# Second mixture-of-experts layer: a routed job's transposes one job later, its down product two jobs later, and three dense slices ahead instead of four

## The chip, the cores and the metric

The kernel runs on one core of a Trainium2 chip. The time is device microseconds (us) of one execution; a kernel's time is the median of several runs. TensorE is written PE (its weight loads PEld), VectorE DVE, ScalarE ACT, GpSimd POOL, and SyncE, which issues the weight transfers, SP.

## The reference, cut to what matters

The whole reference is a stack of two two-layer blocks on 256 tokens of width 1024, in float32. Only its last stage is touched here: a mixture of eight SwiGLU experts of inner width 2816, of which each token uses its two best.

```python
def _moe_swiglu(x, router_w, w_gate, w_up, w_down):
    logits = (t @ router_w).astype(jnp.float32)
    top_vals, top_idx = lax.top_k(logits, TOP_K)          # TOP_K = 2
    w = jax.nn.softmax(top_vals, axis=-1)
    combine = jnp.einsum('nk,nke->ne', w, jax.nn.one_hot(top_idx, N_EXPERTS_2, ...))
    out = jnp.zeros_like(t)
    for e in range(N_EXPERTS_2):                          # 8 experts
        out = out + combine[:, e:e + 1] * _swiglu(t, w_gate[e], w_up[e], w_down[e])
# _swiglu: (silu(x @ w_gate) * (x @ w_up)) @ w_down
```

After it come the residual and a layer norm, and then the output.

## The kernel before, in words

`moe2` (L1621) does this stage. Each expert is cut into `NSL` = 11 slices of 256 inner columns. A slice needs three pieces of weights of 1 MB each: gate, up and down. A *job* is one slice of one expert, written `(r, s)`; there are 88 jobs, so 264 pieces.

Expert 0 is *dense*: it is computed for all 256 tokens (`r` is None). The other seven are *routed*: they are ranked at run time by how many tokens chose them (`route2`), and rank r is computed for a fixed number of gathered tokens. Ranks 0 to 2 (`HEAVY` = 3) take 128 tokens, rank 3 takes 64, ranks 4 to 6 (the *small* ones) take 32. What is left over is added in a branch at the end (`rest2`). Dense and heavy jobs split each weight half into a high and a low part (ACT at L102, DVE at L104, tile `whl`, a ring of six halves) and multiply three times; rank 3 and the small ones use the loaded weights as they are.

`jobs2` writes out the order of the jobs: `DENSE2` dense slices first, then the ranks in the order `SEQ2` = 4, 0, 5, 1, 6, 2, 3, with `AMONG2` dense slices spread among the slices of a rank: four among rank 4 and three among rank 5.

A job has three steps. `up` is the gate and up product with SiLU (ACT) and the product of the two (DVE; L1652 and L1653 for heavy ranks, L1662 and L1663 for the others, tile `sh`; L1372 and L1373 for a dense slice, tile `fh`). `hid`, for a routed job only, transposes the hidden rows on TensorE (L1672, L1681, L1683) and copies them out of PSUM (tiles `shh` and `shl`, or `lhT` at L1685). `down` is the down product into accumulators (tile `sy`, for a dense slice `fy`). Before, the loop issues for job j: `up(j)`, then the extra work tied to that slice, then `down(j-1)`, then `hid(j)`. The extra work is `scatter` of the rank before (slices 1 to 4, tile `scps`), `select` and `gather` for the next rank (slices 5, 7 and 8, tile `gps`), and `rows` (slice 6, tile `slps`).

The PSUM tiles of `up`, `hid`, `scatter`, `gather` and `rows` come from a pool `pg` of two banks that are handed out in turn (a dense `up` takes both). The tiles `fh`, `fhh` and `fhl`, which hold hidden rows and their transposes, have two buffers each.

Three things set the order of work. First, `chunks2` lists the weight pieces in the order in which the steps use them, and SP issues the loads in that order, through a ring of `N_RAW` = 12 buffers. Second, a routed expert's address needs its index: SP reads it at run time (`index2`, L1589), and waits there until `route2` has computed it (L1554). Third, the framework's scheduler fixes the order of instructions in each engine's queue when the kernel is built, from its own estimate of when each will be ready; it prefers the order of the code but fills what it takes for a wait with later work. On the chip each queue then runs strictly in that order.

Of the kernel before, what the change touches and what calls it, by code (L numbers as in the profile page):

```python
# [9 lines left out]
F32 = mybir.dt.float32  # L10
# [10 lines left out]
D = 1024  # L21
# [4 lines left out]
NSL = F2 // 256  # L26
# [3 lines left out]
POOL = tuple(map(int, "0021001000012221112220221210"))  # L30
LAG = 2

DENSE2, HEAVY, SMALL, CAP3 = 4, 3, 4, 32

SEQ2, AMONG2 = (4, 0, 5, 1, 6, 2, 3), (4, 0, 3, 0, 0, 0, 0)
RSQ = (1024 / 27) ** 2
BRANCH = [ET.PE, ET.DVE, ET.Activation, ET.SP]

# [185 lines left out]
class Kern:  # L224
# [1367 lines left out]
    def jobs2(self):  # L1592
# [6 lines left out]
                out.append((r, s))  # L1599
        return out  # L1600

    def chunks2(self, jobs):

        w = self.a["w_moe2"]

        def chunk(r, j):
            if r is None:
                return w[0, j], 2, False
            if callable(r):
                return w[r(), j], 2, False  # L1610
            return (lambda: w[bass.ds(self.index2(r), 1), j].rearrange("o p f -> (o p) f")), 2, r >= HEAVY

        c = []
        for i, (r, s) in enumerate(jobs):
            c += [chunk(r, 2 * s), chunk(r, 2 * s + 1)]
            if i:
                c.append(chunk(jobs[i - 1][0], 2 * NSL + jobs[i - 1][1]))
        c.append(chunk(jobs[-1][0], 2 * NSL + jobs[-1][1]))
        return c

    def moe2(self, stream, x, xt, began, ln, out):  # L1621
# [4 lines left out]
        with ExitStack() as st:  # L1626
# [37 lines left out]
                return h  # L1664

            def hid(r, s, h):
                if r is None:
                    return h
                if r < HEAVY:
                    ps = pg.tile([128, 2, 128], F32, name="shT", tag="fgu")  # L1670
                    for j in range(2):
                        nc.tensor.transpose(ps[:, j, :], h[:, half(j)], self.ident)  # L1672
                    hh = w2.tile([128, 2, 128], F32R, name="shh", tag="fhh")
                    hl = w2.tile([128, 2, 128], F32R, name="shl", tag="fhl")
                    self.split(hh, hl, ps)
                    return hh, hl
                n = size(r)
                ps = pg.tile([128, 2, n], F32, name="lT", tag="fgu")
                if r < SMALL:
                    for j in range(2):  # L1680
                        nc.tensor.transpose(ps[:, j, :], h[hi, half(j)], self.ident[hi, hi])  # L1681
                else:
                    nc.tensor.transpose(ps.rearrange("p j n -> p (j n)"), h[hi], self.ident[hi, hi])  # L1683
                hT = w2.tile([128, 2, n], F32, name="lhT", tag="fhh")
                nc.scalar.activation(hT, ps, AF.Copy)  # L1685
                return hT
# [40 lines left out]
            def select(r):  # L1727
                n = size(r)
                if r in small:
                    m = len(small)  # L1730
                    sel[r] = w2.tile([128, 2, m, n], F32, name="sel", tag="sel", bufs=1)
                    for t in range(2):
                        nc.vector.tensor_tensor(sel[r][:, t], self.iota[:, None, :n].to_broadcast([128, m, n]),
                                                pms[:, t, SMALL:, None].to_broadcast([128, m, n]), op=OP.is_equal)
                    sel[r] = sel[r].rearrange("p t m n -> p t (m n)")
                    t = w2.tile([128, 8, m * n], F32, name="xq", bufs=1)
                    for e in small:
                        xe[e] = t[:, :, half(e - SMALL, n)]
                    xe["small"] = t
                    return  # L1740
                sel[r] = w2.tile([128, 2, n], F32, name="sel", tag="sel", bufs=1)
                for t in range(2):
                    nc.vector.tensor_scalar(sel[r][:, t], self.iota[:, :n], pms[:, t, r:r + 1], None, op0=OP.is_equal)
                if r < HEAVY:
                    xe[r] = w2.tile([128, 8, 2, CAP2], F32R, name="xe", tag="xe", bufs=1)
                else:
                    xe[r] = w2.tile([128, 8, CAP1], F32, name="xl", tag="xl", bufs=1)

            def gather(r, q):
                n, m = sel[r].shape[-1], 4 if r < HEAVY or r in small else 8  # L1750
                ps = pg.tile([128, m, n], F32, name="gps", tag="fgu")
                for k in range(m):
                    for t in range(2):
                        self.mm(ps[:, k], x[:, t, half(m * q + k)], sel[r][:, t], t == 0, t == 1)
                v = xe["small" if r in small else r][:, half(q, m)]
                if r < HEAVY:
                    self.split(v[:, :, 0], v[:, :, 1], ps)
                else:
                    nc.scalar.activation(v, ps, AF.Copy)
# [10 lines left out]
            def scatter(r, t, c):  # L1770
                ps = pg.tile([128, 512], F32, name="scps", tag="fgu")
                for i in range(2):
                    spread(r, i, t, c, ps, i == 0)
                v = pre[:, t, half(c, 512)]
                nc.vector.tensor_tensor(v, v, ps, op=OP.add)

            pend = None
            for r, s in self.jobs2():
                if r == SEQ2[0] and s == 0:
                    select(r)  # L1780
                    for q in range(2):
                        gather(r, q)
                if r == last and s == 2:
                    gb = w2.tile([128, 2, D], F32, name="lngb", tag="xe", bufs=1)
                    gb = self.load_ln(ln, (gb[:, 0], gb[:, 1]), nc.scalar)
                h = up(r, s)
                b = before.get(r)
                b = "small" if b == small[-1] else None if b in small else b
                if b is not None and 1 <= s < 5:
                    scatter(b, (s - 1) // 2, (s - 1) % 2)  # L1790
                n = after.get(r)
                if n is not None and n not in small:
                    if s == 5:
                        select(n)
                    if s in (7, 8) and (n < HEAVY or s == 7):
                        gather(n, s - 7)
                if s == 6 and r is not None and r not in small[:-1]:
                    rows("small" if r in small else r)
                if r == last and s == 8:
                    bank = self.four(p0)  # L1800
                    for t in range(2):
                        for c in range(2):
                            self.mm(bank[t][c], self.ident, pre[:, t, half(c, 512)], True, False)
                if pend is not None:
                    down(*pend)
                pend = (r, s, hid(r, s, h))
            down(*pend)
            for i in range(2):
                for t in range(2):
                    for c in range(2):  # L1810
# [326 lines left out]
```

## Time and profile before

| | |
|---|---|
| median of three runs | 1993.34 us (1990.16 to 1996.72) |
| the profiled execution | 1993.39 us, with a span of 1991.6 us from its first to its last instruction |
| TensorE busy | 1866.9 us, 94% of the span |
| VectorE, ScalarE, GpSimd busy | 891.0, 732.0 and 302.5 us |
| bytes moved | 589.24 MB, 296 GB/s on average |
| TensorE's work in the second mixture-of-experts layer, from the second dense slice on | 1264.3 to 1973.4 us of the span |

Busy time of TensorE is modelled from pipelined matmuls, so a busy TensorE is not one at its peak. What a wait is worth depends on whether the weights or the products set the pace in that stretch, so the layer is read rank by rank.

### The profile page before, as it was taken

How to read it: one execution, taken by the hardware profiler on the slowest of the kernel's cores; microseconds unless marked ns; L12 is line 12 of the kernel's file. 1: busy time of each engine (PE TensorE's matmuls, PEld its weight loads, DVE VectorE, ACT ScalarE, POOL GpSimd, SP SyncE). 2: the span in 40 equal slices, each digit the busy share in tenths (PEclk: the TensorE clock that was granted, in tenths of full speed). 3: DMA queues.
4: the chain of work that ended last, by engine and by line, in shares of the span. 5: the costliest groups of instructions: out<-in, count | busy, mean ns of one | idle time of the engine just before them, and what ended most of it. 6: DMA issues, size and time to landing. Idle time of an engine off the chain costs nothing. (4 is left out here: it accounts for less than half of the span.)

```text
span 1991.6 us, 35592 instructions
## 1 busy us (share of the span) xinstructions
PE 1866.9 (94%) x14962; PEld 1470.1 (74%) x14962; DVE 891.0 (45%) x1609; ACT 732.0 (37%) x1177; POOL 302.5 (15%) x132
## 2 busy tenths in 40 slices
PE   9999999899999998998999999999999989979996
PEld 8885555488655555988999767988898779758953
DVE  5481111267411113476111576633586249628822
ACT  5431111054211112553444372533565247516611
POOL 0210000002000001524888234200000000000000
PEclk9899999999999998999999999999999999999998
DMA  9559999855598993744552431669998999999995
GB/s 383 194 202 402 408 419 419 327 193 191 196 412 328 371 419 117 283 186 158 191 189 94 181 115 64 254 258 389 419 388 312 407 419 388 351 418 419 378 384 208
DMA packets 86027, 589.24 MB, mean 296 GB/s; under 512 B 9782, under 2 KB 11510, under 8 KB 16340
## 3 DMA queue, kind: packets, MB, share of 16 engines
q1 hardware_dynamic: 83042, 580.67, 73.4%
q10 hardware_dynamic: 2802, 6.06, 0.9%
q8 instruction: 124, 2.03, 0.4%
q14 instruction: 59, 0.48, 0.1%
HBM read 585.45 MB, written 1.24 MB: 295 GB/s over the span
## 5 line engine op out<-in xcount | busy, mean ns | idle before, releaser
L102 ACT ACTIVATE whl<-raw 128x1024 fp32r<-128x1024 f32 x426 | 431.3, 1054 | 229.5 <-issue 104.2
L104 DVE TENSOR_TENSOR whl<-raw,whl 128x1024 fp32r<-128x1024 f32 x313 | 373.6, 1234 | 160.2 <-ACT whl L102 152.8
L104 POOL TENSOR_TENSOR whl<-raw,whl 128x1024 fp32r<-128x1024 f32 x113 | 278.1, 2478 | 902.4 <-ACT whl L102 819.1
L282 PE MATMUL fgu<-xh,whl 128*128 128x256 f32 x1280 | 234.8, 284 | 3.6 <-DVE whl L104 1.5
L282 PE MATMUL sgu<-whl,xe 128*128 128x256 f32 x1584 | 198.0, 284 | 10.4 <-ACT whl L102 5.8
L282 PEld LDWEIGHTS fgu<-xh,whl 128*128 128x128 f32 x1280 | 200.9, 192 | 6.0 <-DVE whl L104 1.9
L282 PEld LDWEIGHTS sgu<-whl,xe 128*128 128x128 f32 x1584 | 190.1, 191 | 13.7 <-ACT whl L102 6.9
L282 PE MATMUL fgu<-xl,whl 128*128 128x256 f32 x640 | 180.9, 283 | 0.0
L282 PE MATMUL gu<-raw,xe 128*64 128x256 f32 x1408 | 172.4, 382 | 0.0
L282 PEld LDWEIGHTS gu<-raw,xe 128*64 128x64 f32 x1408 | 102.0, 137 | 53.7 <-issue 5.1
L282 PEld LDWEIGHTS fgu<-xl,whl 128*128 128x128 f32 x640 | 122.8, 192 | 0.6
L282 PE MATMUL zps<-xh,whl 128*128 128x256 f32 x576 | 111.5, 291 | 2.2 <-ACT xh L271 1.4
L282 PE MATMUL fy<-whl,fhh 128*128 128x512 f32 x352 | 111.7, 398 | 0.0
L1860 POOL TENSOR_TENSOR pre<-pre,lngb 128x512 f32<-128x512 f32 x2 | 2.5, 1266 | 701.0 <-ACT pre L1859 701.0
L983 ACT ACTIVATE h<-gu 128x256 f32<-128x256 f32 x31 | 11.9, 385 | 253.6 <-PE gu L282 253.6
L1373 DVE TENSOR_TENSOR fh<-fh,fgu 128x512 f32<-128x512 f32 x20 | 13.8, 688 | 183.5 <-PE fgu L282 183.4
L984 DVE TENSOR_TENSOR h<-h,gu 128x256 f32<-128x256 f32 x31 | 13.1, 421 | 184.8 <-ACT h L983 184.8
L282 PEld LDWEIGHTS zps<-xh,whl 128*128 128x128 f32 x576 | 92.7, 195 | 3.9 <-ACT xh L271 1.6
L282 PE MATMUL yps<-raw,hT 128*64 128x512 f32 x352 | 89.5, 595 | 0.0
L282 PE MATMUL sy<-whl,shh 128*128 128x512 f32 x264 | 84.2, 402 | 3.6 <-ACT whl L102 2.5
L282 PE MATMUL zps<-xl,whl 128*128 128x256 f32 x288 | 82.6, 287 | 1.0 <-DVE xl L272 1.0
L282 PEld LDWEIGHTS fy<-whl,fhh 128*128 128x128 f32 x352 | 64.7, 188 | 15.9 <-issue 1.2
(469 smaller groups left out, 3049.4 us busy)
## 6 DMA issues: line engine op xcount, KB each, us to landing
raw<-in_w_moe_dram SPq DMA_DIRECT2D x399, 1024.0 KB, 9.7
whl<-in_w_moe_dram SPq DMA_DIRECT2D x57, 1024.0 KB, 10.9
raw<-in_w_dense_dram SPq DMA_DIRECT2D x53, 1024.0 KB, 7.1
raw<-in_w_ffn_dram SPq DMA_DIRECT2D x33, 1024.0 KB, 5.9
lngb<-in_lnp_dram ACTq DMA_DIRECT2D x8, 512.0 KB, 4.4
lngb<-in_lnp_dram SPq DMA_DIRECT2D x8, 512.0 KB, 5.1
xraw<-in_xT_dram SPq DMA_DIRECT2D x4, 256.0 KB
raw<-in_w_dense_dram SPq DMA_DIRECT2D x2, 512.0 KB, 4.5
```

The source lines that it names most:

```text
L102: nc.scalar.activation(hi, r, AF.Copy)
L104: on.tensor_tensor(lo, r, hi, op=OP.subtract)
L282: self.nc.tensor.matmul(out, lhsT, rhs, start=start, stop=stop, skip_group_check=True)
L983: nc.scalar.activation(h, ps[:, 0, :], AF.Silu)
L984: nc.vector.tensor_tensor(h, h, ps[:, 1, :], op=OP.mult)
L1373: nc.vector.tensor_tensor(h, h, g[1], op=OP.mult)
L1860: nc.gpsimd.tensor_tensor(v, v, gb[0][:, half(c, 512)], op=OP.mult)
```

## The change

The order of steps is now made by a new function, `steps2`, that both the loop and `chunks2` follow. For job j it issues: `up(j)`; then `down(j-2)` if that job was routed; then, for job j-1, `hid` if it is routed or `down` if it is dense; then the extra work of slice j (`more`). So a routed job's transposes come one job later than its gate and up product and its down product two jobs later; a dense slice's down product still comes one job later. The scatter of the rank before moves to slices 2 to 5. The weight pieces are loaded in the new order of use. The leading dense slices go from four to three, and four stand among rank 5 in place of three.

```diff
-DENSE2, HEAVY, SMALL, CAP3 = 4, 3, 4, 32
-SEQ2, AMONG2 = (4, 0, 5, 1, 6, 2, 3), (4, 0, 3, 0, 0, 0, 0)
+DENSE2, HEAVY, SMALL, CAP3 = 3, 3, 4, 32
+SEQ2, AMONG2 = (4, 0, 5, 1, 6, 2, 3), (4, 0, 4, 0, 0, 0, 0)
...
+    def steps2(self, jobs):
+        out, turned, last = [], None, None
+        for j in [*jobs, None, None]:
+            out += [("up", *j)] if j else []
+            out += [("down", *turned)] if turned else []
+            turned = None
+            if last is not None:
+                if isinstance(last[0], int):
+                    turned = last
+                out.append(("hid" if turned else "down", *last))
+            out += [("more", *j)] if j else []
+            last = j
+        return out
...
-        for i, (r, s) in enumerate(jobs):
-            c += [chunk(r, 2 * s), chunk(r, 2 * s + 1)]
-            if i:
-                c.append(chunk(jobs[i - 1][0], 2 * NSL + jobs[i - 1][1]))
-        c.append(chunk(jobs[-1][0], 2 * NSL + jobs[-1][1]))
+        for step, r, s in self.steps2(jobs):
+            if step == "up":
+                c += [chunk(r, 2 * s), chunk(r, 2 * s + 1)]
+            elif step == "down":
+                c.append(chunk(r, 2 * NSL + s))
...
-                if b is not None and 1 <= s < 5:
-                    scatter(b, (s - 1) // 2, (s - 1) % 2)
+                if b is not None and 2 <= s < 6:
+                    scatter(b, (s - 2) // 2, (s - 2) % 2)
...
-                if pend is not None:
-                    down(*pend)
-                pend = (r, s, hid(r, s, h))
-            down(*pend)
+            gb, bank, hidden = [], [], {}
+            for step, r, s in self.steps2(self.jobs2()):
+                if step == "up":
...
+                    hidden[r, s] = up(r, s)
+                elif step == "hid":
+                    hidden[r, s] = hid(r, s, hidden[r, s])
+                elif step == "down":
+                    down(r, s, hidden.pop((r, s)))
+                else:
+                    more(r, s)
```

## Rows read from the trace of the kernel before

**Rows 1.** The page: its span, and the loads of expert weights (size, landing).
```profile
span 1991.6 us, 35592 instructions
...
raw<-in_w_moe_dram SPq DMA_DIRECT2D x399, 1024.0 KB, 9.7
```

**Rows 2.** Busy time by stretch: length, PE, PEld, DVE, ACT, POOL, clock, DMA share, GB/s.
```profile
1264.30:1307.70 43.40, 43.40 (x298) 40.06 (x296) 20.39 (x19) 18.94 (x21) 7.29 (x3) 1.00 0.75 299
1307.70:1423.80 116.10, 112.69 (x1412) 96.92 (x1411) 39.60 (x49) 35.60 (x56) 0.00 (x0) 1.00 0.92 367
...
1525.70:1626.40 100.70, 93.20 (x1217) 77.59 (x1215) 36.48 (x49) 27.42 (x48) 0.00 (x0) 0.99 0.94 381
...
1725.90:1790.80 64.90, 48.58 (x934) 34.09 (x933) 14.80 (x32) 12.18 (x31) 0.00 (x0) 0.97 0.98 396
1790.80:1895.30 104.50, 101.29 (x729) 93.12 (x729) 85.81 (x93) 70.58 (x90) 0.00 (x0) 0.98 0.95 391
1895.30:1973.40 78.10, 74.79 (x496) 38.46 (x494) 12.53 (x23) 11.33 (x28) 0.00 (x0) 1.00 0.88 357
```

**Rows 3.** What SP waited for, 1190 to 1304 us: total, times, longest.
```profile
SPq L1589 <- DVE idxi L1554: 62.3, 1, 62.3
```

**Rows 4.** Busy time by stretches of 20 us, columns as in rows 2.
```profile
1290.00:1310.00 20.00, 20.00 (x195) 18.58 (x194) 8.86 (x10) 8.58 (x11) 0.00 (x0) 1.00 0.51 186
...
1790.00:1810.00 20.00, 16.04 (x118) 14.28 (x119) 13.34 (x14) 12.13 (x19) 0.00 (x0) 0.91 1.01 419
```

**Rows 5.** Timeline of DVE among the leading dense slices: start, length, instruction.
```profile
1282.43 0.68 DVE L1373 TENSOR_TENSOR fh<-fh,fgu 128x512 f32<-128x512 f32 x1
...
1299.53 0.68 DVE L1373 TENSOR_TENSOR fh<-fh,fgu 128x512 f32<-128x512 f32 x1
```

**Rows 6.** What PE waited for in rank 4, 1304 to 1424 us.
```profile
PE lT L1683 <- DVE sh L1663: 2.7, 3, 2.4
...
PE fgu L282 <- ACT lhT L1685: 0.3, 1, 0.3
```

**Rows 7.** What PE waited for in rank 5, 1526 to 1640 us.
```profile
PE lT L1683 <- DVE sh L1663: 3.0, 4, 0.7
...
PE gps L282 <- ACT lhT L1685: 0.6, 2, 0.3
PE scps L282 <- ACT lhT L1685: 0.6, 2, 0.3
```

**Rows 8.** What PE waited for in rank 6, 1725 to 1800 us.
```profile
PE lT L1683 <- DVE sh L1663: 8.1, 11, 0.8
...
PE sgu L282 <- DMA raw<-in_w_moe_dram: 0.9, 1, 0.9
```

**Rows 9.** What PE waited for in rank 3, 1893 to 1975 us.
```profile
PE scps L282 <- ACT lhT L1685: 1.1, 3, 0.4
...
PE slps L837 <- ACT lhT L1685: 0.4, 1, 0.4
```

**Rows 10.** Timeline of PE in rank 5, up to a dense slice; idle time in brackets.
```profile
1558.71 1.96 PE L282 MATMUL sgu<-raw,xq 128*32 128x128 f32 x64
1561.40 0.27 PE L1683 MATMUL lT<-consts,sh 64*128 64x64 f32 x1 [0.74 <-DVE sh L1663]
1561.61 1.07 PE L282 MATMUL sy<-raw,lhT 128*32 128x256 f32 x16
1562.93 0.38 PE L282 MATMUL fgu<-xh,whl 128*128 128x256 f32 x1 [0.26 <-ACT whl L102]
...
1564.19 0.50 PE L282 MATMUL fgu<-xh,whl 128*128 128x256 f32 x2 [0.76 <-DVE whl L104]
```

**Rows 11.** Timeline of one heavy job's transposes in rank 2.
```profile
1812.29 0.38 PE L1672 MATMUL shT<-consts,sh 128*128 128x128 f32 x2
...
1813.33 0.42 DVE L272 TENSOR_TENSOR shl<-shT,shh 128x256 fp32r<-128x256 f32 x1
```

**Rows 12.** Scatter products within rank 2: durations in ns (minimum, median, maximum).
```profile
L282 PE MATMUL scps<-sy,sT x8: 393/396/505, 1805.2 to 1836.4; 128*128 128x512 f32 x8
```

More of the change, by code (lines that the diff above doesn't have):

```diff
@@ L1666, in hid @@
             def hid(r, s, h):
-                if r is None:
-                    return h
                 if r < HEAVY:
@@ L1775, in scatter, with more @@
                 nc.vector.tensor_tensor(v, v, ps, op=OP.add)
[L1777 to L1786, printed above, removed]
+            def more(r, s):
                 b = before.get(r)
                 b = "small" if b == small[-1] else None if b in small else b
-                if b is not None and 1 <= s < 5:
-                    scatter(b, (s - 1) // 2, (s - 1) % 2)
+                if b is not None and 2 <= s < 6:
+                    scatter(b, (s - 2) // 2, (s - 2) % 2)
                 n = after.get(r)
@@ L1799, in moe2 @@
                 if r == last and s == 8:
-                    bank = self.four(p0)
+                    bank.extend(self.four(p0))
                     for t in range(2):
@@ L1803, in moe2 @@
                             self.mm(bank[t][c], self.ident, pre[:, t, half(c, 512)], True, False)
-                if pend is not None:
-                    down(*pend)
-                pend = (r, s, hid(r, s, h))
-            down(*pend)
+            gb, bank, hidden = [], [], {}
+            for step, r, s in self.steps2(self.jobs2()):
+                if step == "up":
+                    if r == SEQ2[0] and s == 0:
+                        select(r)
+                        for q in range(2):
+                            gather(r, q)
+                    if r == last and s == 2:
+                        v = w2.tile([128, 2, D], F32, name="lngb", tag="xe", bufs=1)
+                        gb = self.load_ln(ln, (v[:, 0], v[:, 1]), nc.scalar)
+                    hidden[r, s] = up(r, s)
[5 more added lines that the diff above has]
+                    more(r, s)
             for i in range(2):
```

## The prediction

> **What bounds the kernel now.** I read the page for its span and the size of a weight load [rows 1], then busy time rank by rank through the layer that changes [rows 2], then what SP waited for, since it feeds the weights [rows 3], then what TensorE waited for in each rank [rows 6 to 9], and last the timeline where a wait needed its cause [rows 5, 10, 11]. The reader should see two things. First, TensorE is the bound of most stretches: in the leading dense slices it is busy for all of 43.4 us, in rank 4 for 112.69 of 116.1, in rank 5 for 93.2 of 100.7, in rank 2 for 101.29 of 104.5 [rows 2]. The transfers there are at 0.75 to 0.95 of their time because the ring is full. Second, rank 6 is the exception: TensorE is busy for 48.58 of 64.9 us while the transfers run at 0.98 [rows 2], and at its end TensorE waits 0.9 us for a weight load itself [rows 8]. At full share the transfers move 419 GB/s [rows 4], so a piece of 1024 KB [rows 1] takes 2.50 us and the three of a job 7.5. A wait that ends in rank 6 is therefore worth little; one that ends in ranks 4, 5, 2 or 3 is worth itself, as long as the ring holds pieces.
>
> The sum is made against the profiled execution, 1993.39 us (its span of 1991.6 and 1.8 around it); the median, 1993.34, is the same within 0.05.
>
> **The dense slice that is moved.** Ahead of the routed ranks a dense slice costs the time between two hidden products, 1299.53 - 1282.43 = 17.1 us [rows 5], with no idle TensorE [rows 2]. Taken out: -17.1. Put among rank 5 it costs the same 17.1 of TensorE time, and an entry: a dense slice after small jobs waits 0.26 and 0.76 us for the split of its first half [rows 10], so +18.1. Below, it could enter for nothing (+17.1); above, with the 0.74 in front of its neighbour's transposes too (+18.8). I take +18.1, as its three sisters do. Net +1.0 us.
>
> What hides the loads: SP stops at the first routed piece until the index is there, 62.3 us [rows 3]. With four leading slices 11 pieces lie ahead of that point (eight gates and ups, three downs), with three only 8, so three pieces (7.5 us) are loaded later, behind the wait. The cover is the full ring: from 1290 to 1310 us the transfers run at 0.51, idle for 9.8 us [rows 4], and the whole stretch at 0.75, idle for 10.9 [rows 2]. Of the first pieces that rank 4 needs none is late: the wait ends at the same time, and TensorE still has two dense slices to do. If that cover were gone, +7.5.
>
> **The transposes one job later.** In rank 4 TensorE waits 2.7 us for `sh` in front of transposes and 0.3 behind a copy of them [rows 6]; in rank 5 3.0, 0.6 and 0.6 [rows 7]. With another job between, both inputs are long there. But two of the four waits in rank 5 (1.5 us) stand right ahead of a dense slice, whose weights are split meanwhile [rows 10]: with the transposes out of the way TensorE waits as long for the split. So -(3.0 + 4.2 - 1.5) = -5.7; from 0, if the scheduler leaves the transposes where they are, to -7.2.
>
> **What takes the place of that wait.** The step after a dense slice has no older routed job to bring down, since the dense one is brought down at once. So in each group of small jobs behind a dense slice there is one place where `up`, `hid` and the next `up` stand with nothing between. With two banks in turn, the second `up` wants the bank that the first one filled, which is free only when SiLU and product have read it. The uncovered chain is the 0.74 us of [rows 10], less the transpose of 0.21 (1561.61 - 1561.40): 0.53 us. There are eight dense slices among ranks 4 and 5: +4.2 us; below, 0.
>
> **Scatters in rank 2.** The old order puts a down product between the scatter and the transposes; the new one runs transposes, scatter, next `up`. The next `up` wants the bank of the transposes, free when `shl` has read it: 1813.33 + 0.42 - 1812.29 = 1.46 us after they start [rows 11]. Under it lie the transposes themselves and a scatter of two products of 0.396 at the median [rows 12], by my estimate 0.5 us at the least, as products overlap. That leaves up to 0.9 us, four times: 0 to +3.6. I take +2.0, nearer the middle, as VectorE is 82% busy here [rows 2] and its place in the queue decides. Scatters in the small ranks copy with ACT alone and cost nothing more.
>
> At one place the Trainium skill speaks against the change: "Perfetto Trace Analysis", section "Matmuls", says that independent groups of products should go round different PSUM banks, so that one is emptied under the next. The traces agree in kind, with the waits of 0.3 us behind a copy of transposes [rows 6]. By that rule alone this and the part above would cost 7.8 us.
>
> **Rank 6 and the start of rank 2.** The 8.1 us of waits in front of transposes [rows 8] lie under the transfers, so they are worth nothing. What can help is the order of the pieces: a gate and up now stand one piece further ahead of a down product, so rank 2's first products can start up to 2.5 us sooner. 0 to -2.5; I take half, -1.25.
>
> **Rank 3 and the end.** Its waits behind a copy of transposes, 1.1 and 0.4 us [rows 9], go, as the scatter now has a free bank: -1.5. At the end two down products follow the last `up` in place of one, and one more copy stands uncovered, +0.4 (the size of the one in [rows 9]). Together -1.1, from 0 to -1.5.
>
> **The sum.** +1.0 - 5.7 + 4.2 + 2.0 - 1.25 - 1.1 = -0.85 us: 1992.5. The rest costs nothing: no product, split or load is added or dropped, and the scatter's shift by one slice keeps its work.
>
> **The rivals.**
>
> *The waits simply end.* No bank stands in the way, the entry of the fourth slice is hidden, and ranks 4, 5 and 3 and the start of rank 2 give all they have: -(3.0 + 4.2 + 2.5 + 1.5) = -11.2, 1982.2. For it: the waits are real and on TensorE. Against it: two banks.
>
> *Rank 5 is bound by its weights.* Then a dense slice there costs its pieces alone, 7.5 us, in place of 18.1: 1992.5 - 10.6 = 1981.9. For it: the transfers run at 0.94 there. Against it: TensorE is busy for 93.2 of 100.7 us [rows 2] and waits for no load [rows 7]. The Trainium skill has the idea behind it: "Perfetto Trace Analysis", section "Optimization Strategy", would interleave stretches with different bounds; in rank 5 the rows bear that out only in small part.
>
> *Slower: the split of the next weights queues behind the late copy.* Each engine runs its queue strictly in order, and the buffers of the transposed rows are two. The copy `lhT` of a job can run only when the down product two jobs older has left its buffer. If the scheduler puts the split of a dense or heavy rank's first half behind that copy, TensorE waits for it longer by one down product, 1.07 us [rows 10]. There are 8 entries to dense slices and 3 to heavy ranks: +11.8, 2004.3. It decides from 0.6 us per entry on. For it: in [rows 10] the split already comes behind the copy. Against it: a split that is ready may be put first.
>
> *The change doesn't do what it says.* The scheduler already departs from the code: in [rows 10] the transposes run ahead of a down product that the code issues first. If it puts them back behind `up`, the waits stay, no bank wait is added, and only +1.0 is left: 1994.4.
>
> **How the numbers follow.** 0.3% of this time, 6 us, is about what a measurement can tell from no change. My forecast and the last rival, both within it, have 0.42; the waits simply ending 0.18 and the weights setting rank 5's pace 0.13, both faster; the queue behind the copy 0.27. So faster 0.31, the same 0.42, slower 0.27. The likeliest case's own range is 1987 to 1999. For 8 in 10 the range reaches to both faster cases and to the slower one: 1980 to 2005.
>
> **What the profile after would show.** The first routed gate 17 us earlier, SP's wait for the index longer but ending at the same time, and no load awaited in rank 4. Rank 5 some 18 to 19 us longer than its 100.7. In ranks 4 and 5 fewer waits of transposes for `sh`, and in their place waits of `sgu` for `sh` of about 0.5 us, once for each dense slice. In rank 2, up to four waits of `sgu` for `shl`. Rank 6 as long as before within 2.5 us. The prediction is wrong if rank 5 grows by less than 12 us, if the waits at the entries of dense slices grow to over 1.6 us, or if TensorE waits for loads in rank 4.

## The result and the profile after

The changed kernel takes 2010.47 us at the median (2005.79 to 2014.66, 4 runs), against 1992.79 us for the kernel before: a ratio of 1.0084, with a 95% interval of 1.0062 to 1.0106. It is 17.7 us slower, above the forecast of 1992.5 and above the range up to 2005. The profiled execution is the slowest of the four, 2014.66 us; its span, 21.3 us above that of before, stands below, so the lengths of its ranks overstate the loss by 3.6 us. First the page's span line, then busy time by stretch, with the columns of [rows 2]. After the page's line: the last leading dense slices, then ranks 4, 0, 5, 1, 6, 2, 3, each cut from the first gate product of the rank to that of the next.

```profile
span 2012.9 us, 35611 instructions
...
1262.90:1289.70 26.80, 26.80 (x182) 24.54 (x180) 13.34 (x12) 11.90 (x14) 4.89 (x2) 1.00 1.01 419
...
1289.70:1405.80 116.10, 111.97 (x1398) 96.76 (x1397) 39.24 (x49) 35.50 (x57) 0.00 (x0) 1.00 0.94 378
1405.80:1498.60 92.80, 92.80 (x694) 85.14 (x693) 76.42 (x82) 64.25 (x84) 0.00 (x0) 1.00 1.00 389
1498.60:1633.00 134.40, 119.23 (x1407) 99.40 (x1406) 50.43 (x63) 40.67 (x64) 0.00 (x0) 0.99 0.86 342
1633.00:1732.10 99.10, 95.22 (x692) 86.78 (x692) 80.88 (x86) 67.44 (x87) 0.00 (x0) 0.98 0.95 364
1732.10:1801.70 69.60, 54.27 (x930) 37.64 (x929) 15.92 (x32) 13.10 (x33) 0.00 (x0) 0.90 0.98 394
1801.70:1910.10 108.40, 102.57 (x734) 92.90 (x734) 83.95 (x91) 69.02 (x88) 0.00 (x0) 0.97 0.89 362
1910.10:1996.20 86.10, 81.56 (x517) 42.08 (x516) 16.08 (x27) 13.69 (x31) 0.00 (x0) 1.00 0.82 337
```

Cut in the same way, the ranks of both kernels and of three experiments (described below) have these lengths in us:

| | first routed gate at | rank 4 | 0 | 5 | 1 | 6 | 2 | 3 | dense slices in rank 5 |
|---|---|---|---|---|---|---|---|---|---|
| before | 1307.7 | 116.1 | 94.7 | 107.9 | 99.5 | 63.6 | 105.8 | 79.6 | 3 |
| after | 1289.7 | 116.1 | 92.8 | 134.4 | 99.1 | 69.6 | 108.4 | 86.1 | 4 |
| e5, after with own banks | 1288.4 | 111.1 | 98.3 | 129.0 | 98.0 | 66.7 | 106.1 | 79.4 | 4 |
| e9, before with own banks | 1306.5 | 113.7 | 95.1 | 107.5 | 97.7 | 65.0 | 105.7 | 76.3 | 3 |
| e17, e9 with the scatter one slice later | 1307.6 | 113.7 | 95.2 | 106.0 | 98.8 | 68.2 | 107.5 | 77.1 | 3 |

From before to after, the first routed gate moves 18.0 us ahead, ranks 4 and 0 together give 1.9, and then rank 5 takes 26.5 more, rank 6 6.0, rank 2 2.6 and rank 3 6.5: 21.3, the difference of the two spans. (Rank 1 gives 0.4.) Of the 26.5, about 17.1 ([rows 5]) are the dense slice that was moved there. Some of the lengths is only carried over a border, as two down products now wait at the end of a rank in place of one: TensorE's time on `sy` is 3.75 us more in rank 6 (17.61 before, 21.36 after) and 3.18 more in rank 3 (30.17, 33.35). (A part of the 3.75 is a lower clock, below.) Carried work costs nothing over the whole layer.

What TensorE waited for in the layer changed in kind. These are rows of the view of waits over the whole stretch from the first routed gate to the last product, first of the kernel before (1307.7 to 1974.9 us):

```profile
PE lT L1683 <- DVE sh L1663: 14.5, 19, 2.4
...
PE scps L282 <- ACT lhT L1685: 2.6, 8, 0.4
...
PE gps L282 <- ACT lhT L1685: 1.3, 4, 0.3
...
PE slps L837 <- ACT lhT L1685: 0.7, 2, 0.4
```

and of the kernel after (1289.7 to 1996.2 us):

```profile
PE scps L282 <- DVE sh L1679: 4.9, 7, 0.7
...
PE lT L1697 <- DVE sh L1679: 3.6, 5, 0.7
PE lT L1695 <- DVE pre L1789: 3.1, 4, 0.8
...
PE gps L282 <- DVE sh L1679: 2.5, 4, 0.7
...
PE lT L1697 <- DVE xe L272: 2.2, 2, 1.2
PE sgu L282 <- DVE fh L1373: 2.0, 2, 1.5
...
PE lT L1697 <- DVE pre L1789: 1.6, 2, 0.8
PE lT L1697 <- DVE slscr L842: 1.1, 1, 1.1
PE sgu L282 <- DVE shl L272: 1.1, 2, 0.7
```

The waits of transposes for their input `sh` fell by 10.9 us, as the change means to have it. But all the other rows shown have nothing to do with data: a scatter does not read `sh`, nor do transposes read `pre` or `xe`. What is awaited is the read that frees one of the two banks of `pg`; in e5, where the transposes have banks of their own, the waits of this kind come to 2.9 us. The rows shown here are 4.6 us before and 18.5 after, 13.9 more. Left out are the waits for splits of weights, 16.0 us before and 20.5 after.

Not all of the loss is waiting. Busy time over the whole stretch, for before, for e2 (the old order with the dense slices of after, described below) and for after:

```profile
1307.70:1974.90 667.20, 626.99 (x6242) 519.54 (x6241) 355.30 (x421) 297.89 (x433) 0.00 (x0) 0.99 0.95 379
```
```profile
1289.80:1979.40 689.60, 651.44 (x6362) 542.05 (x6361) 363.40 (x429) 303.61 (x441) 0.00 (x0) 0.98 0.94 374
```
```profile
1289.70:1996.20 706.50, 657.63 (x6362) 540.69 (x6361) 362.92 (x429) 303.67 (x441) 0.00 (x0) 0.98 0.92 365
```

TensorE is idle for 40.2, 38.2 and 48.9 us. With the same dense slices, the new order adds 10.7 us of idle time and 6.2 of busy time (after against e2).

Two places show how the banks cost time. In rank 3, after (timeline of TensorE, and below it one row of VectorE), the transposes take the bank of the scatter and wait until the scatter's sum `pre` has been read out of it; this stands four times in the rank, 0.78 us here and 3.1 us in all:

```profile
1939.29 0.74 PE L282 MATMUL scps<-sy,sT 128*128 128x512 f32 x2
1940.81 0.27 PE L1695 MATMUL lT<-consts,sh 64*128 64x64 f32 x1 [0.78 <-DVE pre L1789]
```
```profile
1940.06 0.69 DVE L1789 TENSOR_TENSOR pre<-pre,scps 128x512 f32<-128x512 f32 x1 [1.55 <-PE scps L282]
```

The Trainium skill, "Perfetto Trace Analysis", section "Optimization Strategy", reads the same gap repeated on the engine that should be full as a possible sign that there is not enough SBUF or PSUM for the next tile. The four gaps, 3.1 us together, agree with it.

In rank 4, after, a small gate product follows the transposes behind a dense slice and wants a bank of the dense product. VectorE has first put a split of weights of 1.23 us in front of the product `fh` that frees it, so the wait is 1.49 us (TensorE, then VectorE):

```profile
1308.90 0.27 PE L1697 MATMUL lT<-consts,sh 64*128 64x64 f32 x1
1310.66 1.96 PE L282 MATMUL sgu<-raw,xq 128*32 128x128 f32 x64 [1.49 <-DVE fh L1373]
```
```profile
1308.66 1.23 DVE L104 TENSOR_TENSOR whl<-raw,whl 128x1024 fp32r<-128x1024 f32 x1 [1.48 <-ACT whl L102]
1309.92 0.69 DVE L1373 TENSOR_TENSOR fh<-fh,fgu 128x512 f32<-128x512 f32 x1
```

### The profile page after: what moved, and what is told of

It is laid out like the page before. It is cut to its first block, busy times and chain, and to the rows that moved or that the text cites. A ratio compares the mean times of both kernels' runs of the same rounds, so it can differ in the third digit from the quotient of the medians.

```text
span 2012.9 us, 35611 instructions
## 1 busy us (share of the span) xinstructions
PE 1879.9 (93%) x14962; PEld 1476.1 (73%) x14962; DVE 891.1 (44%) x1610; ACT 730.3 (36%) x1177; POOL 299.9 (15%) x131
## 5 line engine op out<-in xcount | busy, mean ns | idle before, releaser
L102 ACT ACTIVATE whl<-raw 128x1024 fp32r<-128x1024 f32 x426 | 430.4, 1053 | 208.9 <-issue 78.6
L282 PE MATMUL sgu<-whl,xe 128*128 128x256 f32 x1584 | 202.5, 286 | 10.7 <-DVE whl L104 5.2
L282 PEld LDWEIGHTS sgu<-whl,xe 128*128 128x128 f32 x1584 | 192.4, 193 | 17.4 <-DVE whl L104 6.6
L1373 DVE TENSOR_TENSOR fh<-fh,fgu 128x512 f32<-128x512 f32 x20 | 13.7, 687 | 183.0 <-PE fgu L282 182.9
```

Source lines behind the costliest of these rows:

```text
L102: nc.scalar.activation(hi, r, AF.Copy)
L282: self.nc.tensor.matmul(out, lhsT, rhs, start=start, stop=stop, skip_group_check=True)
L1373: nc.vector.tensor_tensor(h, h, g[1], op=OP.mult)
```

## The experiments

Ratios are to runs of the kernel before on the same chip, with 95% intervals; the medians come from several chips, so the ratios are what to compare.

| run | order | dense slices ahead | banks | median us | ratio |
|---|---|---|---|---|---|
| after | late | 3 | two | 2010.47 | 1.0084 [1.0062, 1.0106] |
| e1 | late | 4 | two | 2013.96 | 1.0102 [1.0086, 1.0118] |
| e2 | old | 3 | two | 1995.92 | 1.0008 [0.9999, 1.0018] |
| e3 | late, copy `lhT` on VectorE | 3 | two | 2012.62 | 1.0088 [1.0072, 1.0104] |
| e4 | late | 3 | own for `lT` | 2002.48 | 1.0037 [1.0024, 1.0049] |
| e5 | late | 3 | own | 1997.12 | 1.0016 [0.9992, 1.0040] |
| e6 | down product late alone | 3 | two | 2017.97 | 1.0106 [1.0050, 1.0163] |
| e7 | late, weights split one step further ahead | 3 | two | 2011.10 | 1.0088 [1.0061, 1.0115] |
| e8 | old, the same | 4 | two | 1993.17 | 0.9992 [0.9966, 1.0018] |
| e9 | old | 4 | own | 1984.99 | 0.9955 [0.9942, 0.9968] |
| e10 | late | 4 | own | 1992.77 | 1.0007 [0.9994, 1.0021] |
| e11 | transposes late alone | 4 | own | 1998.32 | 1.0021 [1.0009, 1.0033] |
| e12 | down product late alone | 4 | own | 1996.42 | 1.0015 [1.0004, 1.0027] |
| e13 | transposes late alone | 4 | two | 2015.48 | 1.0108 [1.0090, 1.0127] |
| e14 | late, extra work right behind `up` | 4 | two | 2009.31 | 1.0082 [1.0062, 1.0102] |
| e15 | old, extra work at the end of the step | 4 | two | 2000.40 | 1.0034 [1.0023, 1.0045] |
| e16 | late, extra work right behind `up` | 4 | own | 1996.22 | 1.0011 [1.0000, 1.0023] |
| e17 | old, scatter at slices 2 to 5 | 4 | own | 1992.96 | 1.0000 [0.9988, 1.0011] |
| e18 | late, scatter at slices 1 to 4 | 3 | two | 2010.89 | 1.0093 [1.0075, 1.0110] |

### The two halves of the change (e1, e2)

e1 is the kernel after with the dense counts of before, e2 the kernel before with those of after.

```diff
e1, to after:
-DENSE2, HEAVY, SMALL, CAP3 = 3, 3, 4, 32
-SEQ2, AMONG2 = (4, 0, 5, 1, 6, 2, 3), (4, 0, 4, 0, 0, 0, 0)
+DENSE2, HEAVY, SMALL, CAP3 = 4, 3, 4, 32
+SEQ2, AMONG2 = (4, 0, 5, 1, 6, 2, 3), (4, 0, 3, 0, 0, 0, 0)
e2: the same lines the other way, in before
```

> The late transposes and down products alone; dense slices as before (four ahead, three among rank 5). Theory A (the late order itself costs: the split of the next weights comes behind the copy of the late transposes in ACT's queue, plus bank waits): most of the change's 17.7 us shows here, 2003 to 2010 us. Rival (the fourth dense slice in rank 5 costs, the late order is free): 1990 to 1996 us.

> The old order of steps; three dense slices ahead and four among rank 5. Theory A: no change beyond one more entry to a dense slice, 1992 to 1996 us. Rival (the dense slice costs): 2003 to 2010 us. If the weights set rank 5's pace: about 1983 us.

The late order alone has the whole loss, 1.0102. The moved dense slice is worth 1.0008 by itself, 1.6 us by the ratio, beside the +1.0 of the sum.

### Is it the split of the next weights, queued behind the late copy? (e3, e7, e8)

```diff
e3, to after:
-                nc.scalar.activation(hT, ps, AF.Copy)
+                nc.vector.tensor_copy(hT, ps)
e7, to after (e8, to before):
+            stream.ahead = 2
```

> The changed kernel with the copy of the transposes of rank 3 and the small ranks on VectorE in place of ScalarE, so that no split of a high part can stand behind it in ACT's queue. Theory A (queue behind the copy): the waits of 1.26 us of the dense down products for the split end, rank 5 shortens from 134.4 us by some 4 us, the whole is 2002 to 2006 us. Rival (banks): no change, 2008 to 2012 us.

> The changed kernel with each split of weights issued one piece earlier in the code (two pieces ahead in place of one), so that the scheduler has it in hand before the copy of the transposes. Theory A (split behind the copy): the waits of TensorE for splits, 8 us in rank 5 with the down products of dense slices among them, shrink to under 4, the whole 2003 to 2007 us. Rival (the split's place is set by the estimate of the load's landing, not by the code): no change, 2008 to 2012 us.

> The kernel before with the same edit, as a control. Theory A: waits for splits at entries to dense slices and heavy ranks, 9 us in all, shrink, 1987 to 1991 us. Rival: no change, 1991 to 1997 us.

The place exists. After, in rank 5, a dense down product waits for its split, which stands behind a late copy (TensorE; ScalarE):

```profile
1585.43 1.76 PE L282 MATMUL fy<-whl,fhh 128*128 128x512 f32 x5 [1.26 <-ACT whl L102]
```
```profile
1584.21 0.22 ACT L1699 ACTIVATE lhT<-lT 128x64 f32<-128x64 f32 x1 [0.74 <-PE lT L1697]
1584.33 2.00 ACT L102 ACTIVATE whl<-raw 128x1024 fp32r<-128x1024 f32 x2
```

But taking the copy off ScalarE shortened these waits from 2.9 to 1.3 us (rank 5, first after, then e3) and the time not at all, 1.0088. Over the whole layer e3 waits 21.0 us for splits, after 20.5: the wait went elsewhere. Splitting further ahead in the code moved neither kernel, but e7 decides nothing, as its waits for splits are those of after (9.0 us inside rank 5, 20.5 in the layer). What bounds this queue is e2: with the same dense slices and the old order it waits 17.4 us for splits, so the queue can hold some 3 us of the loss, not most of it.

```profile
PE fy L282 <- ACT whl L102: 2.9, 3, 1.3
```
```profile
PE fy L282 <- ACT whl L102: 1.3, 3, 0.4
```

### Are the two banks the price? (e4, e5, e9, e10)

e4 gives the transposes of ranks 3 to 6 a bank of their own, one that the kernel holds for other ends and that is free here. e5 does so too for the heavy ranks 1 and 2, in a bank that the dense accumulator has left by then. Nothing else of after is changed. e9 is the same edit in the kernel before, e10 is e5 with four dense slices ahead and three among rank 5.

```diff
-                    ps = pg.tile([128, 2, 128], F32, name="shT", tag="fgu")
+                    ps = (p0.tile([128, 2, 128], F32, name="fy00") if r else pg.tile([128, 2, 128], F32, name="shT", tag="fgu"))
...
-                ps = pg.tile([128, 2, n], F32, name="lT", tag="fgu")
+                ps = self.p_ps.tile([128, 2, n], F32, name="lT", tag="b3")
```

> The changed kernel with the transposes of rank 3 and the small ranks in a PSUM bank of their own (the one that only the heavy ranks' second accumulator uses), so that scatter, gather and the next gate product no longer take turns with them. Bank theory: the waits of transposes for the scatter's add in rank 3 (3.1 us) and for gather's copies in rank 6 (2.2 us) end, with those of gates for dense products in rank 4 (2.0 us): 2001 to 2005 us. Theory A (queue behind the copy): 2007 to 2011 us.

> The run with an own bank for the small ranks' transposes, and besides it an own bank (one of the dense accumulators', idle by then) for the transposes of ranks 1 and 2. Bank theory: rank 2, 109.1 us in the run without it, goes to about 107 (its waits of gates for the split of the transposes, 1.1 us in the changed kernel, and the scatters between), the whole 1999 to 2002 us beside 2002.5. Rival (the heavy ranks lose nothing to banks): no change, 2002 to 2004 us.

> The old order with the banks of its own (transposes of small ranks and rank 3, and of the heavy ranks 1 and 2, out of the two shared banks), four dense slices ahead. Theory (the two shared banks cost the new order its 13 us because it puts gate, transposes and scatter of different jobs next to each other): the old order has a down product between these steps and its waits are for the hidden rows, not for a bank, so own banks give it little: 1988 to 1994 us, ratio 0.998 to 1.000. Rival (own banks are worth some 13 us to any order, so they say nothing about the new one): about 1980 us, ratio 0.993.

> The new order with own banks, but four dense slices ahead and three among rank 5 as in the old order. Theory: late order alone was 1.0102; own banks took 0.68 per cent from the whole change, and the move of one dense slice is worth 0.001 at most, so ratio 1.001 to 1.004, 1995 to 2001 us. Rival (with the banks out of the way the late order shows the gain of up to 11 us that its ended waits promise): 1982 to 1987 us, ratio 0.994 to 0.997.

Own banks take 13.4 us off the changed kernel (2010.47 to 1997.12). Busy time by stretch of e5, ranks 4 and 3:

```profile
1288.40:1399.50 111.10, 111.03 (x1395) 96.22 (x1394) 36.68 (x46) 32.12 (x53) 0.00 (x0) 1.00 0.95 380
...
1897.60:1977.00 79.40, 78.46 (x517) 41.30 (x516) 15.58 (x26) 13.45 (x30) 0.00 (x0) 1.00 0.89 366
```

TensorE no longer idles in rank 4, where it is busy for 111.03 of 111.10 us, and the four gaps of rank 3 are gone, with 6.7 us of its length (3.6 of idle and 3.1 of busy time). Over the layer TensorE is idle for 38.6 us, from 48.9, though the transposes wait for `sh` again for 7.9 us, from 3.6. The place behind the dense slice in rank 4 has no wait (e4, timeline of TensorE):

```profile
1308.47 0.27 PE L1697 MATMUL lT<-consts,sh 64*128 64x64 f32 x1
1308.67 2.15 PE L282 MATMUL sgu<-raw,xq 128*32 128x128 f32 x66
```

What rank 4 gives is not all gained: rank 0 behind it takes 98.3 us in place of 92.8, and ranks 4 and 0 together need 208.9 us after and 209.4 in e5. After, the transfers run at 1.00 of their time in rank 0, so an earlier start may meet weights that can come no earlier; this is argued from the shares, not shown by a run. In e5 TensorE waits there 3.0 us for splits and never for a load.

e9 broke my expectation. I had written that own banks give the old order little; they gave it 0.45%. So the two banks are a price of both orders, and the kernel before with own banks, 1984.99 us, is the fastest that was run. And e10 shows that with own banks the late order still stands 0.5% behind e9. With four dense slices on all sides, the late order costs 1.02% in two banks (e1) and 0.52% with own banks (e10 against e9): the banks hold half of its price.

### Which delay? (e6, e11, e12, e13)

e6 (from after) and e12 (from e10) put the transposes back into their own job and keep the down product two jobs late. e11 (from e10) and e13 (from e1) keep the transposes one job late and put the down product right behind them.

```diff
e6 and e12, in steps2:
-                out.append(("hid" if turned else "down", *last))
+                else:
+                    out.append(("down", *last))
+            out += [("hid", *j)] if j and isinstance(j[0], int) else []
e11 and e13, in steps2:
-            out += [("down", *turned)] if turned else []
-            turned = None
             if last is not None:
                 if isinstance(last[0], int):
-                    turned = last
-                out.append(("hid" if turned else "down", *last))
+                    out.append(("hid", *last))
+                out.append(("down", *last))
```

> The changed kernel with the transposes put back to their own job, behind the down product of two jobs before; the down product stays two jobs late. It parts the late transposes from the late down product. Bank theory (transposes between an older job's scatter and the next gate cost): the order up, down, transposes, scatter still takes turns in two banks, 2005 to 2011 us. If only the transposes being a job late is to blame: 1993 to 1998 us.

> Four dense slices ahead, own banks for the transposes; transposes one job later, but the down product straight behind them, one job late as in the old order (gate and up, transposes of the job before, its down product, extra work). With own banks the old order is at 0.9955 and the whole late order at 1.0007. Theory A (what is left, 0.5 per cent, is the down product's second job of delay: a heavy rank's down product stands in the next small rank, and scatter and gate follow each other): this kernel falls to 0.994 to 0.997, 1981 to 1987 us. Theory B (what is left comes from the late transposes: a copy and the down product that wants it now stand next to each other, some 0.4 us each time): it stays at or above 1.0007, 1993 us or more.

> Four dense slices ahead, own banks; transposes in their own job as in the old order, the down product two jobs late. Theory A (the delay of the down product costs what is left): 0.999 to 1.002, 1991 to 1996 us, like the whole late order with own banks. Theory B (the late transposes cost it): 0.994 to 0.997, 1981 to 1987 us, like the old order with own banks.

> The same order as in e11 (transposes one job late, the down product right behind them), but in the two shared banks; four dense slices ahead. The whole late order in two banks is at 1.0102, the late down product alone (with three slices ahead) at 1.0106. If the banks' price comes from transposes and gate of neighbouring jobs meeting in two banks, this order pays it too: 1.004 to 1.010, 2000 to 2012 us. If it comes from the down product's delay, which takes the work away that lay between two uses of a bank: 0.998 to 1.001, 1988 to 1994 us.

Each delay costs the same alone as both together: 1.0106 and 1.0108 beside 1.0102 in two banks, 1.0015 and 1.0021 beside 1.0007 with own banks. Neither theory A nor B stands. But equal ratios do not prove one cause: in e6 no scatter and no gather waits for `sh`, while transposes wait 16.3 us for `sh` and `sgu` 5.5 for `shl`. The next runs try what all late orders share.

### What all late orders share: the place of the extra work and of the scatter (e14 to e18)

In the new loop scatter, select, gather and rows come at the end of the step, and the scatter comes one slice later.

```diff
e14, to e1, and e16, to e10, in steps2:
             out += [("up", *j)] if j else []
+            out += [("more", *j)] if j else []
...
-            out += [("more", *j)] if j else []
e15, to before: "down(*pend)" and "pend = (r, s, hid(r, s, h))" moved to right behind "h = up(r, s)"
e17, to e9:
-                if b is not None and 1 <= s < 5:
-                    scatter(b, (s - 1) // 2, (s - 1) % 2)
+                if b is not None and 2 <= s < 6:
+                    scatter(b, (s - 2) // 2, (s - 2) % 2)
e18, to after: these two lines the other way
```

> The late order (transposes one job later, down product two) in the two shared banks, four slices ahead, but the extra work (scatter, select, gather, rows) straight behind the gate and up product, as in the old order, in place of at the end of the step. Theory C (all three late orders, whichever step they delay, cost the same 1.0 per cent in two banks and 0.2 with own banks, so the price is in what they share: extra work at the end, with no down product between a scatter and the next gate or the transposes): falls to 0.998 to 1.003, 1988 to 2000 us. Theory D (any delay of transposes or down product costs it): stays at 1.008 to 1.012, 2009 to 2017 us.

> The old order of gate, down product and transposes, nothing delayed, in the two shared banks, with only the extra work moved from straight behind the gate and up product to the end of the step. Theory C: the price appears here without any delay, 1.005 to 1.010, 2002 to 2013 us. Theory D: no change, 0.998 to 1.002, 1988 to 1997 us.

> As e10 (late order, own banks for the transposes, four slices ahead), with the extra work straight behind the gate and up product. Theory C: the half per cent left in e10 against the old order with own banks goes too, 0.994 to 0.998, 1981 to 1989 us. Theory D: as e10, 1.0007, 1992 to 1997 us.

> The old order with own banks (e9, 0.9955), with only the scatter moved one slice later, to slices 2 to 5, as every late order has it. Theory E (the scatter's place, beside select and rows, is what keeps every late order with own banks at 1.0007 to 1.0021): 1.000 to 1.002, 1992 to 1997 us. Theory D (a delay of transposes or down product costs the half per cent by itself): no change from e9, 0.994 to 0.997, 1981 to 1988 us.

> The changed kernel, two shared banks and three slices ahead, with only the scatter put back to slices 1 to 4. In the old order with own banks the shift of the scatter alone cost 0.45 per cent (e17 against e9). Theory E (the shift costs that in the changed kernel too): 1.003 to 1.005, 1998 to 2003 us. Rival F (in two banks the scatter meets the transposes and the gate at either slice, and the banks hold the whole price): 1.007 to 1.010, 2006 to 2013 us.

The place of the extra work costs the old order 0.34% in two banks (e15), but putting it back gives the late order 0.2%, within the two intervals (e14 against e1), and nothing with own banks (e16). The scatter is another matter. With own banks, one slice later costs the old order 0.45% (e17 against e9), nearly as much as parts e10 from e9 (0.52). The two traces reach rank 6 within 0.8 us (1720.5 and 1721.3). There the scatters and the products of `rows` stand apart in e9 (first fence) and run into each other in e17 (second): scatter, scatter, scatter and three of `rows`, each waiting until VectorE has read the one before, with a gate product cut in two around them. The third gate of the rank begins at 1737.15 us in e9 and takes 1.95; in e17 it begins at 1737.08, but ends only at 1745. The third fence, busy time by stretch in e17 and below it in e9, shows two more causes. The granted clock is at its lower level, 0.50, behind these waits, so 60 products take 3.63 us, where e9 needs 1.95 for 64. And the transfers stand still, at 0.04 of their time, as the ring is full: SP waits up to 9.1 us for gates here.

```profile
1734.98 0.74 PE L282 MATMUL scps<-sy,sT 128*128 128x512 f32 x2
1736.50 0.72 PE L282 MATMUL scps<-sy,sT 128*128 128x512 f32 x2 [0.78 <-DVE pre L1775]
1737.15 1.95 PE L282 MATMUL sgu<-raw,xq 128*32 128x128 f32 x64
```
```profile
1736.43 0.72 PE L282 MATMUL scps<-sy,sT 128*128 128x512 f32 x2 [0.78 <-DVE pre L1775]
1737.08 0.41 PE L282 MATMUL sgu<-raw,xq 128*32 128x128 f32 x4
1737.93 0.72 PE L282 MATMUL scps<-sy,sT 128*128 128x512 f32 x2 [0.44 <-DVE pre L1775]
1739.43 0.47 PE L837 MATMUL slps<-consts,slsp 128*128 128x128 f32 x1 [0.78 <-DVE pre L1775]
1740.22 0.47 PE L837 MATMUL slps<-consts,slsp 128*128 128x128 f32 x1 [0.32 <-DVE slsp L835]
1741.02 0.47 PE L837 MATMUL slps<-consts,slsp 128*128 128x128 f32 x1 [0.32 <-DVE slsp L835]
1741.42 3.63 PE L282 MATMUL sgu<-raw,xq 128*32 128x128 f32 x60
```
```profile
1741.40:1745.00 3.60, 3.60 (x62) 2.96 (x61) 0.23 (x1) 0.00 (x0) 0.00 (x0) 0.50 0.04 9
...
1741.40:1745.00 3.60, 2.86 (x85) 2.18 (x77) 0.29 (x1) 0.49 (x2) 0.00 (x0) 1.00 0.99 401
```

In the profiled executions rank 6 is 3.2 us longer and rank 2 1.8, 5.0 of the 6.7 between the two spans. The 1.8 is not shown to be the scatter's: the granted clock of rank 2 is 0.95 in e17 and 0.98 in e9, and the same 730 products keep TensorE busy 2.7 us longer. The late orders with own banks show the same mark: in e10, e11, e12 and e16 rank 6 takes 68.5 to 68.9 us with the transfers at 0.91 to 0.93 of their time, in e9 65.0 at 0.97, and in e10 too a gate is cut in two between the scatters and `rows`. No run puts their scatter back.

In the changed kernel itself, with its two banks, the same line undone gives nothing: e18 stands at 1.0093. There the scatters' waits for `sh` fall from 4.9 to 2.7 us and those of rank 3's transposes for `pre` from 3.1 to 1.6, but the waits for splits rise from 20.5 to 22.7.

## Why the prediction was wrong, point by point

The sum had -0.85 us; the profiled execution has +21.3. Rank by rank the miss is largest in rank 5 (+26.5; the sum had +18.1 for the dense slice, -2.7 for waits that end and +2.1 for banks, together +17.5), rank 3 (+6.5, for -1.1) and rank 6 (+6.0, for -1.25).

**The dense slice and its cover: right.** The first routed gate comes 18.0 us earlier, for 17.1. SP's wait for the index is 17.5 us longer than in [rows 3] (from 1180 us on), no load is awaited in rank 4, and the leading slices run with the transfers at 1.01, the ring being filled there. e2 gives the move +1.6 us by its ratio, for +1.0.

```profile
SPq L1589 <- DVE idxi L1554: 79.8, 1, 79.8
```

**The transposes' own waits: right in kind.** Waits of `lT` for `sh` are gone in rank 4 (2.7 us in [rows 6]) and 0.7 in rank 5 (3.0 in [rows 7]). That their end is worth 5.7 us no run shows: with own banks, too, the late order is slower (e10 against e9).

**What takes the place of that wait: this is the step that failed.** I let only `up` meet `up` in the two banks, at eight places of 0.53 us, and put +4.2. That wait, `sgu` for `sh`, does not occur once in the layer after. Measured in ranks 4 and 5: 2.0 (`sgu` for `fh`, up to 1.5 each, as a split stood in front of `fh`), 1.3 (`fgu` and `sgu` for a copy), and in rank 5 2.0, 1.0 and 1.6 (`scps` and `gps` for `sh`, `lT` for `pre`), 7.9 together. Over the whole layer the rows of waits for banks shown above rose by 13.9 us, where the sum had 4.2 and 2.0. The wrong sentence is that scatters in the small ranks "copy with ACT alone and cost nothing more". I counted the copy of the transposes; but the scatter's own bank is freed by VectorE's sum into `pre`, and the gate's bank by the product `sh`. With the down product gone from between these steps, each of them stands in front of the next step. The Trainium skill's rule that independent groups of products rotate through PSUM banks ("Perfetto Trace Analysis", section "Matmuls") pointed the right way: the 7.8 us that the prediction worked out beside it, for this and rank 2 together, is nearer to the 9.8 of the trace than the 6.2 of the sum.

**"The rest costs nothing": wrong too.** Against e2, which has the same dense slices, TensorE is busy 6.2 us longer and waits 3.1 us more for splits. What the busy time is made of stays open.

**Rank 2: right in size.** +2.6 us, for +2.0; the waits are `sgu` for `shl`, 1.1, as forecast, and `shT` for `pre`, 0.8, which was not.

**Rank 3: the wrong sign.** The forecast was -1.1, "as the scatter now has a free bank". The scatter has; the transposes behind it have not: 3.1 us of waits for `pre`, where there were 1.5 behind a copy in [rows 9]. Of the 6.5 us more, 3.2 are carried down products; with own banks 6.7 go, 3.6 of them idle time.

**Rank 6 and the start of rank 2: wrong.** In place of 0 to -2.5 the rank is 6.0 us longer. The granted clock is 0.90 there, from 0.97 in [rows 2], and 3.75 us are carried down products, but the transfers ran at 0.97 (before, cut at the gates, below) and 0.98 of their time, so they set the pace, and rate times length gives 25.2 and 27.4 MB. That is two pieces more, by my estimate some 5 us at the 419 GB/s of [rows 4]. Why they came so late stays open.

```profile
1725.90:1789.50 63.60, 48.16 (x933) 33.87 (x932) 13.51 (x31) 11.29 (x31) 0.00 (x0) 0.97 0.97 396
```

**The scatter's shift "keeps its work": it has a price that two banks hide.** It costs the old order 0.45% with own banks (e17), and undoing it in two banks gives nothing (e18).

**The rivals.** *The split behind the late copy*, 2004.3, came nearest in time, but for another reason: e3 takes the copy out of that queue, and the time stays. *The waits simply end*, 1982.2, did not come with own banks either: rank 4 then has no idle TensorE, but the whole stays at 1.0016 (e5). *Rank 5 bound by its weights* did not come: the transfers there fell to a share of 0.86, from 0.94. *The change doesn't do what it says* fell too: the waits for `sh` did end.

**How much of the 0.84% is the banks'?** Three counts are possible. For the late order alone, with four dense slices on all sides, it is half: 1.02 points in two banks, 0.52 with own banks. Taken off the changed kernel, own banks are worth 0.68 of the 0.84 points, more than any other edit that leaves the order late. But they give the old order 0.45 as well, so with own banks on both sides the change still costs about 0.6% (1.0016 against 0.9955). Of this 0.6, 0.1 is the moved dense slice (e5 against e10), and the scatter's later place is able to cost 0.45 (e17). That it does so in the late order with own banks is likely from rank 6 of those traces, but no run puts it back; this stays open. Also open is a part of the busy time: after, TensorE is busy some 13 us longer in the layer than before, besides the dense slice, and only up to 7 of that can be the lower clock (27.3 us at the lower level in these ranks, 13.6 before). Against e2, with 30.6 us at the lower level, the 6.2 us are none of the clock's. e3 lost as much with 13.6 us at the lower level, so the clock is not the cause.

## What to carry to other kernels

Before a step is delayed, list which of the shared PSUM tiles are asked for in the new order, one behind the other, and for each who reads it last and what stands in front of that reader in its queue; the work taken from between two steps was also what hid the emptying of a bank. Give the cheap tiles (here the transposes) a bank of their own first: that alone made the old order 0.45% faster, while the reordering in two banks lost 0.84%. When every variant of a reordering costs about the same, compare their waits before you take one cause for all: here e6 waited for other things than the changed kernel, and the side job that all of them moved by one slice had a price only with own banks. And before you read a stretched product as a wait, read the granted clock of that stretch.

## What was not expected of the hardware

TensorE's granted clock fell to its lower level (0.50, which is 1.2 of 2.4 GHz) for a longer time in rank 6 after the change: 0.90 on average, 0.97 in [rows 2]. Two stretches of after, from the view of busy time:

```profile
1738.20:1741.60 3.40, 3.40 (x12) 2.18 (x15) 0.35 (x1) 0.23 (x1) 0.00 (x0) 0.51 1.04 398
1772.30:1782.50 10.20, 8.33 (x91) 5.77 (x92) 1.21 (x4) 0.49 (x2) 0.00 (x0) 0.50 1.01 418
```

The first lies in the carried down products, right behind two waits of 0.5 us for splits. One product of that kind takes 0.63 us there and 0.40 in the next carried job, at the full clock (timeline of TensorE):

```profile
1740.92 0.63 PE L282 MATMUL sy<-whl,shl 128*128 128x512 f32 x1
...
1748.41 0.40 PE L282 MATMUL sy<-whl,shl 128*128 128x512 f32 x1
```

In the second stretch the transfers run at 1.01, so less is lost. The time at the lower level in rank 6 went from 3.4 to 13.7 us among the profiled executions of all kernels here, with no firm tie to the order: e3 and e18, as slow as after, had 3.4.
